# Loads of shrinking size through one ring, in a row-maximum kernel

## The chip, the core and the metric

The kernel runs on one core of one Trainium2 chip. The metric is the device time of one execution in microseconds (us). Several executions are made of each kernel, and kernels that are compared run in turns on the same chip. The profile of an execution gives its *span*, from the first to the last instruction of the program; in the runs below the time is 1.7 to 2.0 us longer than the span of the same execution. Where the text says faster or slower, it means that the 95% interval leaves out 1, or it compares medians and says so.

## The reference

```python
def setup_inputs():
    batch, seq, dim = 32, 512, 1024
    return {"x": np.random.randn(batch, seq, dim).astype(np.float32)}

def reference(x):
    return np.max(x, axis=-1).astype(np.float32)
```

The input is 67 MB, the output 64 KB: 16,384 rows of 1024 floats, each reduced to its maximum. A kernel lays 128 rows in a line on each of the 128 partitions, so "one row" below means one row on every partition, 128 x 4 KB = 0.52 MB, and the whole work is 128 such rows.

## The kernel before

```python
    GB = 4
    GT = 2
    TAIL_ROWS = 16
    ...
    bulk = ctx.enter_context(tc.tile_pool(name="bulk", bufs=10))
    tailp = ctx.enter_context(tc.tile_pool(name="tailp", bufs=5))
    ...
    for c in range(NB):                      # 28 loads of four rows
        b = c * GB
        xc = bulk.tile([P, GB, D], mybir.dt.float32)
        nc.sync.dma_start(out=xc, in_=xr[:, b:b + GB, :])
        nc.vector.reduce_max(out=res[:, b:b + GB], in_=xc, axis=mybir.AxisListType.X)

    nc.scalar.dma_start(out=out_r[:, :SPLIT], in_=res[:, :SPLIT])

    for t in range(NT):                      # 8 loads of two rows
        b = SPLIT + t * GT
        xt = tailp.tile([P, GT, D], mybir.dt.float32)
        nc.sync.dma_start(out=xt, in_=xr[:, b:b + GT, :])
        nc.vector.reduce_max(out=res[:, b:b + GT], in_=xt, axis=mybir.AxisListType.X)

    nc.scalar.dma_start(out=out_r[:, SPLIT:], in_=res[:, SPLIT:])
```

The sync engine (SP) issues the loads, the vector engine (DVE) takes the maxima, the scalar engine (ACT) issues two stores. The framework adds the semaphore waits.

## Time and profile before

| | before |
|---|---|
| time, median of runs | 166.98 us (166.93 to 167.51) |
| span of the profiled execution | 166.5 us |
| DVE busy | 141.4 us, 85% |
| load queue busy | 95.7% of sixteen DMA engines |
| loads | 36: 28 of four rows, 8 of two |

The page and the views that matter are shown in the prediction. One more pair of lines is needed for what follows. It is from the timeline of the vector engine in the kernel before (start in us, duration, engine and line, operation, and in brackets how long the engine had stood idle and what it waited for):

```profile
22.90 4.42 DVE L47 TENSOR_REDUCE res<-xc 128x4 f32<-128x4096 f32 x1 [0.47 <-DMA xc<-in_x_dram]
...
28.43 4.42 DVE L47 TENSOR_REDUCE res<-xc 128x4 f32<-128x4096 f32 x1 [1.11 <-DMA xc<-in_x_dram]
```

The usual wait for a four-row load is 0.47 us. The load that is taken up at 28.43 came 0.64 us late: a stall of the load stream. There is a second one of 0.86 us at 58.61. The packet records of the trace show what a stall is (below, a packet counts as stalled that takes 0.25 us longer than the usual one of its size): at 23.1 to 23.7 us, eight of the sixteen DMA engines each need 0.6 to 0.8 us longer than usual for one packet, and at 51.1 to 51.6 us eight need up to 1.8 us longer (the records kept here do not number the engines; eight late packets at once are read as eight engines). The other eight have no late packet. At the first stall the first engine to land stays on time (27.12 us, one usual load of 4.90 us after the 22.22 of the load before); at the second, when the sixteen stood 1.25 us apart, it comes 0.35 us late (56.85, where 51.60 and 4.90 give 56.50), and which engines were struck the records do not say. The load was taken up only when its slowest engine had landed: at 28.43, with the last landing at 28.40, and at 58.61, with the last at 58.59.

### The profile page before, as it was taken

What the parts mean: (1) busy time and instruction counts of PE and PEld (TensorE: products, weight loads), DVE (VectorE), ACT (ScalarE), POOL (GpSimd) and SP (SyncE); (2) the same over time, 40 slices, a digit from 0 to 9 for tenths busy, and PEclk for the clock granted to TensorE, in tenths of its full rate; (3) what the DMA queues carried; (4) which work ended last, traced back from release to release, by engine and by line L of the source; (5) the groups of instructions that cost most, each with busy time, mean ns of one, the idle gap of its engine ahead of it and who ended that gap; (6) DMA issues with size and microseconds to landing.
All of it is one profiled execution on the core that took longest, in us unless ns stands there. A gap on an engine that the chain in (4) does not pass through costs nothing.

```text
span 166.5 us, 142 instructions
## 1 busy us (share of the span) xinstructions
DVE 141.4 (85%) x36; POOL 0.2 (0%) x4
## 2 busy tenths in 40 slices
DVE  0098887898888798888898888899888889999994
POOL 0000000000000000000000000000000000000000
DMA  5999999999999999999999999999999999999950
GB/s 189 429 441 429 429 394 425 433 437 429 433 421 354 425 433 429 429 429 429 433 421 429 429 429 437 417 429 433 429 433 421 425 433 411 425 417 423 421 222 2
DMA packets 5472, 67.18 MB, mean 404 GB/s; under 512 B 864, under 2 KB 864, under 8 KB 864
## 3 DMA queue, kind: packets, MB, share of 16 engines
q1 hardware_dynamic: 5184, 67.11, 95.7%
q10 hardware_dynamic: 288, 0.07, 0.2%
HBM read 67.11 MB, written 0.07 MB: 403 GB/s over the span
## 4 chain that ended last, share of the span: by engine, by line
DMA 89%; DVE 8%; SPq 1%; issue 0%
DMA xc<-in_x_dram 84%; DMA xt<-in_x_dram 5%; DVE res L59 5%; DVE res L47 3%; SPq L46 1%
## 5 line engine op out<-in xcount | busy, mean ns | idle before, releaser
L47 DVE TENSOR_REDUCE res<-xc 128x4 f32<-128x4096 f32 x28 | 123.8, 4420 | 22.5 <-DMA xc<-in_x_dram 22.5
L59 DVE TENSOR_REDUCE res<-xt 128x2 f32<-128x2048 f32 x8 | 17.8, 2280 | 0.2 <-DMA xt<-in_x_dram 0.2
L80 POOL MEMSET const-bfloat16-1.0<- 128x1 bf16 x1 | 0.1, 103 | 0.0
L80 POOL MEMSET const-uint8-127<- 128x1 uint8 x1 | 0.1, 103 | 0.0
L80 POOL MEMSET const-float32-1.0<- 128x1 f32 x1 | 0.1, 100 | 0.0
L80 POOL MEMSET const-float32-0.0<- 128x1 f32 x1 | 0.1, 99 | 0.2 <-issue 0.2
## 6 DMA issues: line engine op xcount, KB each, us to landing
xc<-in_x_dram SPq DMA_DIRECT2D x28, 2048.0 KB, 39.1
xt<-in_x_dram SPq DMA_DIRECT2D x8, 1024.0 KB, 23.5
out_dram<-res ACTq DMA_DIRECT2D x1, 56.0 KB, 6.8
out_dram<-res ACTq DMA_DIRECT2D x1, 8.0 KB, 1.4
```

Source lines behind the costliest of these rows:

```text
L46: nc.sync.dma_start(out=xc, in_=xr[:, b:b + GB, :])
L47: nc.vector.reduce_max(out=res[:, b:b + GB], in_=xc, axis=mybir.AxisListType.X,)
L59: nc.vector.reduce_max(out=res[:, b:b + GT], in_=xt, axis=mybir.AxisListType.X,)
L80: nc = _bacc.Bacc("TRN2", target_bir_lowering=False, num_devices=1)
```

## The change

The intent is to issue fewer and larger loads while there is much to do, and ever smaller ones towards the end, so that little is left to reduce when the last bytes arrive. All loads go through one tile of 46 rows used as a ring.

```diff
+ROWS = [10, 13, 12, 10, 9, 8, 7, 7, 6, 5, 5, 4, 4, 3, 3, 3, 3, 2, 2, 2, 2, 2, 1, 1, 1, 1, 1]
+RING = 46
...
-    bulk = ctx.enter_context(tc.tile_pool(name="bulk", bufs=10))
-    tailp = ctx.enter_context(tc.tile_pool(name="tailp", bufs=5))
+    ring = once.tile([P, RING, D], F32)
+    res = once.tile([P, I], F32)
+    part = once.tile([P, 2], F32)
...
+    for g in ROWS:
+        if at + g > RING:
+            at = 0
+        xc = ring[:, at:at + g, :]
+        nc.sync.dma_start(out=xc, in_=xr[:, b:b + g, :])
+        nc.vector.reduce_max(out=res[:, b:b + g], in_=xc, axis=X)
+        at += g
+        b += g
+        if not stored and b >= I - 16:
+            stored = b
+            nc.scalar.dma_start(out=out_r[:, :b], in_=res[:, :b])
...
+    for h in range(2):
+        xh = ring[:, at, h * H:(h + 1) * H]
+        nc.sync.dma_start(out=xh, in_=xr[:, b, h * H:(h + 1) * H])
+        nc.vector.reduce_max(out=part[:, h:h + 1], in_=xh, axis=X)
+    nc.vector.tensor_tensor(
+        out=res[:, b:b + 1], in0=part[:, 0:1], in1=part[:, 1:2],
+        op=mybir.AluOpType.max,
+    )
+    nc.scalar.dma_start(out=out_r[:, stored:], in_=res[:, stored:])
```

(The two old loops are cut from the diff; they stand above.)

More of the change, by code (lines that the diff above doesn't have):

```diff
@@ L7 @@
 from concourse._compat import with_exitstack
+F32 = mybir.dt.float32
+ROWS = [10, 13, 12, 10, 9, 8, 7, 7, 6, 5, 5, 4, 4, 3, 3, 3, 3, 2, 2, 2, 2, 2, 1, 1, 1, 1, 1]
+RING = 46
 @with_exitstack
@@ L18 @@
     P = 128
+    X = mybir.AxisListType.X
     xf = x.flatten_outer_dims()
     N, D = xf.shape
-    assert N % P == 0
+    H = D // 2
     I = N // P
@@ L28 @@
     out_r = bass.AP(tensor=of.tensor, offset=of.offset, ap=[[I, P], [1, I]])
-    GB = 4
-    GT = 2
-    TAIL_ROWS = 16
-    NB = (I - TAIL_ROWS) // GB
-    NT = TAIL_ROWS // GT
-    SPLIT = I - TAIL_ROWS
-    bulk = ctx.enter_context(tc.tile_pool(name="bulk", bufs=10))
-    tailp = ctx.enter_context(tc.tile_pool(name="tailp", bufs=5))
-    respool = ctx.enter_context(tc.tile_pool(name="res", bufs=1))
-    res = respool.tile([P, I], mybir.dt.float32)
-    for c in range(NB):
-        b = c * GB
-        xc = bulk.tile([P, GB, D], mybir.dt.float32)
-        nc.sync.dma_start(out=xc, in_=xr[:, b:b + GB, :])
-        nc.vector.reduce_max(
-            out=res[:, b:b + GB],
-            in_=xc,
-            axis=mybir.AxisListType.X,
-        )
-    nc.scalar.dma_start(out=out_r[:, :SPLIT], in_=res[:, :SPLIT])
-    for t in range(NT):
-        b = SPLIT + t * GT
-        xt = tailp.tile([P, GT, D], mybir.dt.float32)
-        nc.sync.dma_start(out=xt, in_=xr[:, b:b + GT, :])
-        nc.vector.reduce_max(
-            out=res[:, b:b + GT],
-            in_=xt,
-            axis=mybir.AxisListType.X,
-        )
-    nc.scalar.dma_start(out=out_r[:, SPLIT:], in_=res[:, SPLIT:])
+    once = ctx.enter_context(tc.tile_pool(name="once", bufs=1))
+    ring = once.tile([P, RING, D], F32)
+    res = once.tile([P, I], F32)
+    part = once.tile([P, 2], F32)
+    b = at = 0
+    stored = 0
+    for g in ROWS:
[9 more added lines that the diff above has]
+            nc.scalar.dma_start(out=out_r[:, :b], in_=res[:, :b])
+    assert b == I - 1 and at + 1 <= RING
+    for h in range(2):
[7 more added lines that the diff above has]
+    nc.scalar.dma_start(out=out_r[:, stored:], in_=res[:, stored:])
 _INS = ['x']
```

## The prediction

> **What bounds the kernel now.** I read the page first, then the timeline of the vector engine (DVE), then the chain of waits and the groups. Of the page, the share of each engine, the strip of slices and the queue:
>
> ```profile
> DVE 141.4 (85%) x36; POOL 0.2 (0%) x4
> ...
> DMA  5999999999999999999999999999999999999950
> GB/s 189 429 441 429 429 394 425 433 437 429 433 421 354 425 433 429 429 429 429 433 421 429 429 429 437 417 429 433 429 433 421 425 433 411 425 417 423 421 222 2
> ...
> q1 hardware_dynamic: 5184, 67.11, 95.7%
> ```
>
> The load queue is full from the second slice to two before the last, at about 429 GB/s, so the load stream sets the time; the DVE has only some 25 us to spare over the whole. Two slices (394 and 354 GB/s) show short stalls. The groups give the price of a reduce:
>
> ```profile
> L47 DVE TENSOR_REDUCE res<-xc 128x4 f32<-128x4096 f32 x28 | 123.8, 4420 | 22.5 <-DMA xc<-in_x_dram 22.5
> L59 DVE TENSOR_REDUCE res<-xt 128x2 f32<-128x2048 f32 x8 | 17.8, 2280 | 0.2 <-DMA xt<-in_x_dram 0.2
> ```
>
> Two rows more cost 4420 - 2280 = 2140 ns, so a row is 1.07 us and an instruction has a fixed 0.14 us (4.42 - 4 x 1.07). The timeline gives the rhythm (start, duration, then in brackets the idle time before):
>
> ```profile
> 132.03 4.42 DVE L47 TENSOR_REDUCE res<-xc 128x4 f32<-128x4096 f32 x1 [0.47 <-DMA xc<-in_x_dram]
> 136.92 4.42 DVE L47 TENSOR_REDUCE res<-xc 128x4 f32<-128x4096 f32 x1 [0.47 <-DMA xc<-in_x_dram]
> 141.82 4.42 DVE L47 TENSOR_REDUCE res<-xc 128x4 f32<-128x4096 f32 x1 [0.48 <-DMA xc<-in_x_dram]
> 146.16 15.47 DVE L59 TENSOR_REDUCE res<-xt 128x2 f32<-128x2048 f32 x7
> ...
> 161.80 2.29 DVE L59 TENSOR_REDUCE res<-xt 128x2 f32<-128x2048 f32 x1 [0.17 <-DMA xt<-in_x_dram]
> 164.12 0.34 ACTq L65 DMA_DIRECT2D out_dram<-res  x1
> ```
>
> In the bulk the DVE waits 0.47 us for each load, so a four-row load takes 4.895 us. In the tail it runs seven two-row reduces without a gap: a backlog, because a four-row reduce holds it 4.42 us while a two-row load lands in about 2.5 us. It has just worked that off when the last load lands at 161.78. Then follow 2.29 us of reduce and 2.4 us of store and ending (164.09 to 166.5). The chain says the same, and what paces the issue of loads:
>
> ```profile
> 102.70 39.10 DMA xc<-in_x_dram
> 141.80 0.02 issue
> 141.82 4.42 DVE res L47
> 146.24 6.59 DVE res L59 x3
> 152.84 0.02 issue
> 152.85 8.93 DMA xt<-in_x_dram
> 161.78 0.02 issue
> 161.80 2.29 DVE res L59
> ```
>
> A load issued at 102.70 lands 39.10 us later, which is 8 x 4.89: eight loads are in flight, and a new one is issued when the load eight before it lands. The end is thus last landing (161.8), plus whatever the DVE has left then (2.29), plus 2.4.
>
> [...]
>
> **The price of a load.** The last four-row load lands at 141.80 and eight two-row loads later it is 161.78: 19.98 / 8 = 2.4975 us each (1.049 MB in that time is 420 GB/s). From 4r + f = 4.895 and 2r + f = 2.4975 follows r = 1.199 us a row and f = 0.10 us a load. All 36 loads are 128 x 1.19875 + 36 x 0.10 = 157.04 us; the last one is taken up at 161.80, so start, latency and the two stalls are 4.76 us. The stalls show as DVE waits of 1.11 us before 28.43 and 1.33 before 58.61, against 0.47: 0.64 + 0.86 = 1.5 us of the 4.76. I keep them.
>
> **The change, part by part.**
> 1. Loads: 27 + 2 = 29 in place of 36. The bytes stay, so 7 x 0.10 = 0.7 us goes, and the last landing is taken up at 161.80 - 0.70 = 161.10. I chose to let f hold for 52 KB and 2 KB pieces per partition, outside the two sizes measured.
> 2. Start of the DVE: the first reduce waits for ten rows, six more than now, so it starts near 8.24 + 6 x 1.2 = 15.4 in place of 8.24. From there 29 reduces back to back are 128 x 1.07 + 29 x 0.05 = 138.4 us (0.05 because a back-to-back one starts before the end of the one before: 2.28 us long, but one each 2.19). That could end at 153.8, so the late start costs nothing; it must only not leave a backlog.
> 3. Backlog: the DVE keeps up from group k to k+1 where 1.07 g(k) + 0.14 stays below 1.199 g(k+1) + 0.10, that is where a size is at least about 0.9 of the one before. The list does that or repeats a size until the backlog is gone. Reckoned through the list, the waits for the DVE stay under 0.8 us; the five two-row loads take up 0.3 us each (2.4975 against 2.19) and clear the backlog of the 3-to-2 step. So the last two-row reduce starts at landing: 161.10 - 5 x 1.299 - 2 x 0.699 = 153.21, and ends at 155.49.
> 4. Tail: one-row loads come each 1.299 us, one-row reduces take 1.07 + 0.14 = 1.21 and 1.12 back to back. Five of them start at 155.40, 156.52, 157.64, 158.76 and 159.88, each behind its landing. The half rows: reduce 0.535 + 0.14 = 0.675, 0.585 back to back. They start at 161.00 and 161.59, the second 0.49 after its data, and end at 162.26. The maximum of the two parts follows: [...] 162.45. So 1.35 us follow the last landing in place of 2.29: of the ideal gain of a half-row end [...] one third is lost to backlog.
> 5. Stores: the first still covers 112 rows, the last 16. The 2.4 us stay.
> 6. Ring: 46 rows in place of 50. For each load I compared the reckoned moment its rows are read out, and that of the landing eight before it, with the moment when the stream would reach it: the smallest spare time is 9.7 us, for the last half row (released by the landing of the twenty-first load, near 150.8, wanted near 160.4). No load should come late.
>
> Sum: DVE end 164.09 to 162.45, 1.64 us less; 166.98 - 1.64 = 165.3 us, about 1.0% faster.
>
> **Rivals.**
> A. The price per load does not fall with their number (larger pieces gain nothing, or pieces of 4 and 2 KB cost more than 0.10 extra). Then the last landing stays at 161.8 and only about 0.9 us of tail is won: 166.0. For it: f comes from two sizes only. Against: in the trace nothing; it is a line through two points that I lengthen.
> B. The DVE becomes the bound at the end: the taper is tuned tight, and if a short reduce had 0.25 us fixed in place of 0.14, seven short ones add 0.11 each, 0.8 us: 166.1. Against: [...] the fixed part that is left over from two sizes should hold for a third.
> C. The stalls shrink, move or fall together. They cost 1.5 us; without them 163.8. For it: the stream's order changes wholly. Against: nothing in the profile ties them to a load or an instruction, and three runs agree within 0.6 us.
> D. The ring is one tile: if overlaps of its parts were tracked as a whole, every load would wait for the reduce before it, loads and reduces would alternate, and the time would be near 157 + 139 = 296. For it: one allocation. Against: the kernel before already writes one result tile in parts and stores a part of it at 146.27 while reduces of later rows are still to come.
>
> **Range and chances.** A and B together would give 166.9, one alone about 166.0; C alone 163.8; a start with larger first pieces may win or lose some tenths. I take 164.2 to 166.4. Faster by over 2% needs 163.6, which takes C and more: 0.06. Slower takes D or an unseen wait: 0.03. Within 2%: 0.91.
>
> **What would show it.** 29 loads and load share near 95%; first reduce near 15.4; four-row and larger groups at 1.07 us a row; the last landing near 161.1; one-row reduces without gaps in the last 7 us, and 1.3 to 1.4 us from last landing to the end of the maximum; last store issued near 162.5. I am wrong if the last landing is not earlier by 0.5 to 0.9 us, if a load waits for the ring so that the strip of slices has a hole, if the stalls are gone, or if the DVE still has a row or more left at the last landing.

162.26 us for the end of the second half row and 0.19 for the maximum with its waiting gave the 162.45, and so the 1.35 us after the last landing, the 1.64 us of gain and the 165.3 us. (In the trace of the change it is 0.20 us from the end of the second half row to the end of the maximum, 162.21 to 162.41.)

## The result, and the profile after

| | before | after |
|---|---|---|
| time, median | 166.98 us (166.93 to 167.51) | 166.44 us (165.94 to 166.67) |
| span of the profiled execution | 166.5 us | 164.7 us |
| DVE busy | 141.4 us | 139.5 us |
| loads | 36 | 29 |

The ratio after to before is 0.9954 (95% interval 0.9934 to 0.9975). Such a ratio is the mean time of one kernel's runs over that of the other's of the same rounds, so it is not quite the ratio of the medians. The change is faster by half a per cent where one per cent was predicted, and 166.44 lies just above the range of 164.2 to 166.4.

The spans tell another story than the times: 1.8 us between the two profiles, 0.5 us between the medians. The four executions of the changed kernel have spans of 164.7, 164.6, 164.2 and 164.9 us, each 1.7 to 1.8 us below its time. By that distance the profiled execution of the kernel before, with its span of 166.5, would have a time near 168.2 us, more than the slowest of its listed times. The profile that I predicted from was thus of an unusually slow execution (an inference from the distance), and the span of a median one would be near 165.2 us.

These lines are from the page of the changed kernel (busy time by engine; the 40 slices; the queue of the loads):

```profile
DVE 139.5 (85%) x30; POOL 0.2 (0%) x4
...
DMA  6998999999989999999999999999999999999960
GB/s 199 438 467 376 453 465 453 436 406 394 469 388 467 444 430 430 408 438 425 439 432 425 426 431 419 428 438 409 438 430 421 427 421 421 420 418 421 408 260 2
...
q1 hardware_dynamic: 4176, 67.11, 95.8%
```

No slice has a hole, so the ring never made a load late. The early slices swing because few packets of 40 and 52 KB fall into a slice of 4.1 us (their medians in this trace are 1.51 and 1.97 us, so two or three an engine); the row of busy shares above them stays at 8 and 9 tenths. Next the timeline of the vector engine, its start and its end:

```profile
15.82 10.82 DVE L48 TENSOR_REDUCE res<-ring 128x10 f32<-128x10240 f32 x1 [15.82 <-DMA ring<-in_x_dram]
31.56 14.02 DVE L48 TENSOR_REDUCE res<-ring 128x13 f32<-128x13312 f32 x1 [4.91 <-DMA ring<-in_x_dram]
...
160.94 1.27 DVE L59 TENSOR_REDUCE part<-ring 128x1 f32<-128x512 f32 x2
162.25 0.16 DVE L60 TENSOR_TENSOR res<-part 128x1 f32<-128x1 f32 x1
162.44 0.34 ACTq L64 DMA_DIRECT2D out_dram<-res  x1
```

The first reduce starts at 15.82, 0.4 us later than predicted; the vector work ends at 162.41, where 162.45 was predicted. And the last part of the chain that ended last (start, length, what):

```profile
133.17 19.92 DMA ring<-in_x_dram
153.08 0.02 issue
153.11 7.92 DVE res L48 x6
161.02 1.20 DVE part L59 x2
162.22 0.02 issue
162.25 0.16 DVE res L60
```

From the landing of the last two-row load at 153.08 to the end, the chain is vector work alone: six reduces, two halves, one maximum, without a gap. The last half row is complete at 160.74, 1.67 us before the vector work ends.

So the profile agrees with the prediction to 0.04 us at the end of the vector work, and yet the gain is half of what was predicted. That is possible because two errors cancel in this one trace. It has only 0.66 us of stall (two packets of the nine-row load are late, and its slowest landing with them), where the prediction carried 1.5 us of stalls over. Something else must have cost what the missing stalls saved.

### The profile page after: what moved, and what is told of

It reads as the page before. It is cut to its first block, busy times and chain, and to the rows that moved or that the text cites. A ratio compares the mean times of both kernels' runs of the same rounds, so it can differ in the third digit from the quotient of the medians.

```text
span 164.7 us, 118 instructions
## 1 busy us (share of the span) xinstructions
DVE 139.5 (85%) x30; POOL 0.2 (0%) x4
## 3 DMA queue, kind: packets, MB, share of 16 engines
q1 hardware_dynamic: 4176, 67.11, 95.8%
## 4 chain that ended last, share of the span: by engine, by line
DMA 70%; DVE 28%; issue 0%
DMA ring<-in_x_dram 70%; DVE res L48 27%; DVE part L59 1%; DVE res L60 0%
## 5 line engine op out<-in xcount | busy, mean ns | idle before, releaser
L48 DVE TENSOR_REDUCE res<-ring 128x2 f32<-128x2048 f32 (+11 forms) x27 | 138.1, 5165 | 22.9 <-DMA ring<-in_x_dram 22.7
L59 DVE TENSOR_REDUCE part<-ring 128x1 f32<-128x512 f32 x2 | 1.3, 676 | 0.0
```

Source lines behind the costliest of these rows:

```text
L48: nc.vector.reduce_max(out=res[:, b:b + g], in_=xc, axis=X)
L59: nc.vector.reduce_max(out=part[:, h:h + 1], in_=xh, axis=X)
```

## The experiments

Theory: without stalls the change gains some 0.9 us and not 1.6, because the start of the stream and the large loads cost more than my line said; the stalls come on top and blur it. Rival: the gain is as predicted, but large loads draw stalls of their own that take it back. Each kernel below, but for the repetitions of the two kernels themselves, is the changed kernel with another list of sizes; those whose list ends with a whole row also lack the two half rows and the maximum of them. Landing times of the single DMA engines are from the semaphore updates in the trace.

### Both kernels again, and each half of the change alone (one chip)

`e1_before` is the kernel before, unchanged.

> The kernel before once more, as the control, to see what its usual execution looks like. The profile that I predicted from had a span of 166.5 us with two stalls (0.64 + 0.86 us) of half of the DMA engines. Theory S (the stalls of that profile are not usual): the time is again 167.0 us, the span about 165.2 (1.75 us less than the time, as in all runs of the changed kernel), a trace has at most about 0.3 us of late landings, the last load lands near 160.4. Rival M (the stalls are usual and the distance of time and span is another for this kernel): span 166.4 to 166.5, the stalls at the same places, last landing 161.8.

Measured: ratio 1.0003, spans 165.5 to 166.4; the trace (166.0) has again two stalls of eight engines each, at 22.9 and at 62.2 us. The first makes later loads land almost 1.0 us late. The second strikes while the engines stand 1.45 us apart, and then they are only 0.84 apart: it hits the engines that were ahead and costs the end nothing. The last load lands at 161.25. The thirteenth load lands at 67.82, where 8.12 of the first and 12 x 4.895 give 66.86, so 0.96 us is what the stalls cost. Taking it off gives 160.29; the first profile gives 161.78 - 1.50 = 160.28. The two agree, so the kernel before **without stalls** has its last landing at 160.28 and a span of 160.28 + 2.29 + 2.40 = 164.97 us. Both theories were half right: stalls are usual, at 23 us even at the same place, but less costly than in the first profile (median span 165.8, so about 0.8 over 164.97).

`e1_after` is the changed kernel again.

> The changed kernel once more. Theory S: its trace held one engine that fell behind by 0.66 us at 65 to 68 us (the load of nine rows: spread of the sixteen engines' landings from 0.89 to 1.56 us) and an early spread of 0.93 against 0.67 us; if that is usual for it, spans are 164.2 to 164.9 again and the last load lands near 160.7 to 160.8, and the true gain is 0.5 to 0.8 us. Rival: that stall was chance; then this trace has none, a span near 164.0, and the list of spans scatters over 0.7 us or more.

Measured: ratio 0.9948 (0.9918 to 0.9979); spans 164.3 to 166.0. The rival expected such scatter, but also a trace without a stall, and this execution (166.0) has one at 62.9 us (five engines, again in the nine-row load) and one at 75.1 us (eight engines, 1.5 to 1.9 us each, in the eight-row load), and its engines end 2.4 us apart. The early spread is there again, 0.90 us.

`e1_tail` keeps four-row loads to row 112 and takes the new tail alone.

```diff
-ROWS = [10, 13, 12, 10, 9, 8, 7, 7, 6, 5, 5, 4, 4, 3, 3, 3, 3, 2, 2, 2, 2, 2, 1, 1, 1, 1, 1]
+ROWS = [4] * 28 + [2, 2, 2, 2, 2, 1, 1, 1, 1, 1]
```

> The new tail alone: loads of four rows to row 112, then 2,2,2,2,2,1,1,1,1,1 and two halves, in the ring of 46. If the backlog reckoning holds, the backlog of the four-row loads is not worked off in so short a tail, the DVE ends as late as before: the same time as before, within 0.3 us (the last landing is 0.3 us later for the five loads more, and the end of the vector work 0.1 us later). If the tail is what gains, 1.0 to 1.4 us less than before.

Measured: ratio 1.0033 (1.0005 to 1.0062), slower by 0.5 us between the means and 0.3 between the medians; the trace has two stalls. Its timeline shows why the fine tail gains nothing:

```profile
142.44 21.02 DVE L48 TENSOR_REDUCE res<-ring 128x4 f32<-128x4096 f32 x11 [0.50 <-DMA ring<-in_x_dram]
...
163.37 1.27 DVE L59 TENSOR_REDUCE part<-ring 128x1 f32<-128x512 f32 x2
```

From the landing of the last four-row load the vector engine runs eleven reduces and then the halves without a gap. 22.4 us after that landing it is done (142.44 to 164.84). In the kernel before it was 22.3 us (141.82 to 164.09). With that backlog before them, the smaller loads did not end sooner.

`e1_bulk` has the large loads alone, with the old tail and no half rows.

```diff
-... 3, 3, 3, 3, 2, 2, 2, 2, 2, 1, 1, 1, 1, 1]      (and the two half rows)
+... 3, 3, 3, 3, 2, 2, 2, 2, 2, 2, 2, 2]
```

> The large loads alone: the first 17 loads of the change (10,13,...,3,3,3,3), then eight loads of two rows as before, in the ring of 46. By the price of a load: 11 loads fewer than before, 0.9 to 1.1 us less stream, and the end follows it by 0.9 to 1.1 us. If large loads bring their own delay (engines that start or fall behind unevenly), the gain is under 0.3 us and the spread of the landings is above 1.2 us.

Measured: ratio 0.9959 (0.9934 to 0.9984), 0.7 us less between the means. The trace has no stall at all, and its chain ends

```profile
160.04 0.02 issue
160.07 2.29 DVE res L48
```

so the last landing is 160.04, only 0.24 us before the 160.28 of the kernel before without stalls. By the prediction's line, eleven loads fewer should have given 1.1 us. Two things took the rest. The stream starts late: the first ten rows land at 15.99, where the landing of the first four rows at 8.22 plus six rows at 1.2 us give some 15.4. And the line itself is off. The two-row loads of this trace are taken up 2.48 us apart (each was waited for, as the brackets say):

```profile
152.64 2.29 DVE L48 TENSOR_REDUCE res<-ring 128x2 f32<-128x2048 f32 x1 [0.17 <-DMA ring<-in_x_dram]
155.12 2.29 DVE L48 TENSOR_REDUCE res<-ring 128x2 f32<-128x2048 f32 x1 [0.20 <-DMA ring<-in_x_dram]
157.60 2.29 DVE L48 TENSOR_REDUCE res<-ring 128x2 f32<-128x2048 f32 x1 [0.19 <-DMA ring<-in_x_dram]
160.07 2.29 DVE L48 TENSOR_REDUCE res<-ring 128x2 f32<-128x2048 f32 x1 [0.18 <-DMA ring<-in_x_dram]
```

The prediction had 2.4975, a mean over eight loads of the kernel before. One of the eight took 2.62 us (it lands at 151.87), the others 2.46 to 2.50. Each of the twenty traces has such a late two-row load, or two that are a little late, while the 144 packets of the first store pass or just after (in the changed kernel the packets start from 147.5 to 150.4 us, and the late load lands at 150.75). In the eight-row kernel below, whose first store is the latest of all, the late load is the latest too (154.71). That the store delays it is read from this coincidence; no run leaves the store out.

With 2.485 us for a two-row load, 4r + f = 4.895 and 2r + f = 2.485 give r = 1.205 us a row and f = 0.075 us a load. That fits loads of all whole rows. Between successive landings in the changed kernel (in brackets the line of 1.205 and 0.075, then the prediction's): 15.73 us for thirteen rows (15.74, 15.68), 14.53 for twelve (14.54, 14.49), 12.12 for ten (12.13, 12.09), 8.51 for seven (8.51, 8.49), 1.28 for one (1.28, 1.30). So in these landings the large loads cost the stream nothing of their own, but for the first one. In this kernel eleven loads fewer are worth 0.83 us, and the late start takes 0.54 of it (15.99 against 8.22 + 6 x 1.205 = 15.45). The 0.29 us that remain are close to the 0.24 measured.

### The start, the end, and both together (another chip)

`e2_start46` cuts the first load in two.

```diff
-ROWS = [10, 13, 12, ...
+ROWS = [4, 6, 13, 12, ...
```

> The first load of ten rows cut into four and six; all else as the change. In the three traces with a ten-row first load it lands at 15.74 to 15.99 us, where my line put 15.35, and the sixteen engines' landings of it are 0.90 to 1.13 us apart against 0.61 to 0.67 for a four-row first load. Theory H (a large first piece costs the start about 0.4 us, for good, since each engine keeps its lag): ten rows are there at 15.4 to 15.5, spread about 0.65, and all later landings 0.3 us earlier than in the change where no stall is; end 0.3 us earlier. Rival (the start is the same for any size, large pieces are slow throughout): ten rows at 15.8 plus 0.1 for the load more, end 0.1 us later.

Measured: ratio 0.9885 (0.9857 to 0.9913). Its timeline:

```profile
8.10 4.42 DVE L48 TENSOR_REDUCE res<-ring 128x4 f32<-128x4096 f32 x1 [8.10 <-DMA ring<-in_x_dram]
15.38 6.55 DVE L48 TENSOR_REDUCE res<-ring 128x6 f32<-128x6144 f32 x1 [2.86 <-DMA ring<-in_x_dram]
...
31.12 14.02 DVE L48 TENSOR_REDUCE res<-ring 128x13 f32<-128x13312 f32 x1 [9.19 <-DMA ring<-in_x_dram]
45.81 12.95 DVE L48 TENSOR_REDUCE res<-ring 128x12 f32<-128x12288 f32 x1 [0.67 <-DMA ring<-in_x_dram]
```

Ten rows are there at 15.36 instead of 15.8, although there is one load more, and thirteen rows later it is 31.09 instead of 31.53. The engines' own landings of the first ten rows:

```
first load            ten rows landed (last engine)      engines apart
ten rows  (6 traces)  15.74 15.78 15.80 15.81 15.97 15.99   0.87 to 1.13
4 + 6     (5 traces)  15.34 15.36 15.36 15.51 15.53         0.45 to 0.74
```

Theory H, that ten rows as one load come about 0.4 us later than as two, agrees with all eleven traces (with the repetitions below). Why is not shown. The sixteen engines begin about 1 us apart, and their first packets take longer than later ones: in the first two profiles on average 0.65 us longer with the 40 KB packets of the change and 0.47 with the 16 KB of the kernel before, which is less than half of the 0.4 us. Nor does all of the gain last. In this trace it was lost again in the loads of twelve and ten rows: row 45 is there at 58.16 us, in the changed kernel at 58.18. So the low ratio of this run is not shown to come from the start. Over the five traces with a split first load, row 45 lands at 57.74 to 58.17, in the six others at 58.13 to 58.40: of 0.43 us on average, 0.27 are left.

`e2_nohalf` keeps the last row whole.

```diff
-    for h in range(2):  ...  nc.vector.tensor_tensor(...)
+ROWS = [..., 1, 1, 1, 1, 1, 1]
```

> The last row as one load and one reduce, in place of two halves and a maximum; all else as the change. Theory B (in the last 7.7 us the vector engine is the bound: six one-row reduces run without a gap from the landing of the last two-row load): from that landing to the end of the vector work 9.30 us in the change becomes 2.29 + 6 x 1.126 + small = 9.05, so 0.25 us less, although the last reduce is twice as long. Rival (the end follows the last landing): the work after the last landing grows from 1.35 to 1.3 or more and the last load lands the same, so no gain or 0.2 us later.

Measured: ratio 0.9894 (0.9871 to 0.9917). The last two-row load lands at 152.42, then

```profile
152.44 9.05 DVE L48 TENSOR_REDUCE res<-ring 128x2 f32<-128x2048 f32 x7 [0.17 <-DMA ring<-in_x_dram]
161.52 0.34 ACTq L56 DMA_DIRECT2D out_dram<-res  x1
```

9.05 us to the end of the vector work, against 9.30 in the change (153.11 to 162.41), as theory B said to the hundredth. (The time fell by more: 166.10 us, against 166.92 for the change in later rounds on the same chip. What is over 0.25 us of that is not explained; the executions of the change scatter by 1.2 us there.) A half row *lengthens* the end by 0.25 us, because the vector engine is the bound there: two short reduces and a maximum take 1.39 us in the change (161.02 to 162.41), and the one whole reduce in their place takes 1.13 here (the last piece of this run's chain). This trace has no stall, and so gives the change without stalls: the same to 152.42, then 0.02 + 9.30 + 2.32 (the end of its own trace, 162.41 to 164.73), a span of 164.06 us.

`e2_best` does both and refines the taper: 4,6,13,12,10,9,8,7,7,6,5,5,4,4,4,3,3,3,2,2,2,2 and seven of one.

> Both, and a finer taper: 4,6,13,12,10,9,8,7,7,6,5,5,4,4,4,3,3,3,2,2,2,2 and seven of one. By the reckoning with the measured prices and no stall: end 0.7 us before the change and 1.6 us before the kernel before, so a ratio to before near 0.990 to 0.991 (the change 0.995). If start and half rows don't matter, 0.995 as the change.

Measured: ratio 0.9842 (0.9822 to 0.9863), median 165.29 us against 167.94, better than expected; spans 163.4 to 163.7. Its end:

```profile
151.21 10.17 DVE L48 TENSOR_REDUCE res<-ring 128x2 f32<-128x2048 f32 x8 [0.20 <-DMA ring<-in_x_dram]
161.41 0.34 ACTq L56 DMA_DIRECT2D out_dram<-res  x1
```

`e2_ring` has the old sizes in the new ring.

```diff
+ROWS = [4] * 28 + [2] * 8
```

> The old sizes (28 loads of four, 8 of two) in the new ring of 46 rows: the form alone. Loads are paced by the landing eight before, so the same time as before, within 0.3 us. On stalls: the three traces with four-row loads had half of the engines late at 23 us (0.5 to 0.9 us), the three with large loads not there. If it belongs to four-row loads, it is here too, at 23.0 to 23.7 us; if it was chance, it is elsewhere or gone.

Measured: ratio 1.0003 (0.9983 to 1.0023). The ring itself does nothing. The trace has two stalls of eight engines again, but the first at 13.4 us and not at 23.

### The change beside its variants, and three-row loads (the same chip again)

Of the thirteen executions of the kernel before in this group, eleven are those of the group above.

> The changed kernel, now in the same rounds as its variants. Without stalls its span is reckoned at 164.0 to 164.1 (first landing 15.8, last two-row landing 152.4, 9.30 us of vector work, 2.35 to the end), against 164.95 for the kernel before: a gain of 0.9 us that stalls blur. Expected ratio 0.993 to 0.996. If its 0.995 of two chips was bad luck with stalls, it comes out at 0.989 like the two half variants.

Measured: ratio 0.9937 (0.9915 to 0.996), as expected; so the 0.995 of the two chips before was not bad luck.

> The split first load once more, beside the change. First look: ten rows at 15.36 as theory H said, but 0.3 us of it lost again in the loads of twelve and ten rows. If H holds: first ten rows at 15.3 to 15.5 again, spread under 0.75, and a time 0.2 to 0.5 us under the change of the same rounds. If the loss in the loads after it belongs to the split: that loss is here again and the time is within 0.2 us of the change.

Measured: ratio 0.989 (0.9864 to 0.9916), median 166.07 against 166.92 for the change: 0.85 us less, more than the start can explain. Ten rows at 15.51 and no loss in the loads of twelve and ten rows this time; but fifteen late packets in the nine-row load at 60 us. The direction is as theory H has it; the size of the gain is not settled by it.

> The best version once more, on another chip and beside the change: ratio to before 0.983 to 0.988, and 0.6 to 1.3 us under the change of the same rounds; list of spans narrower than that of before.

Measured: ratio 0.9872 (0.9848 to 0.9895), 1.3 us under the change (the chip was the same as in the last rounds, not another).

`e3_three`, sizes `[3] * 37 + [2] * 8 + [1]`:

> Loads of three rows (37), then eight of two and one of one, in the ring, for the stalls: all four traces with loads of four rows hold two stalls of eight engines each (mean loss 0.7 to 1.2 us an engine), all between 13 and 63 us; of six traces with large loads one holds two, one a stall of two engines, four none over 0.5 us. Without stalls I reckon 1.0 us more stream than before (ten loads more) and a span of 165.2 to 165.8. If small loads draw stalls, the trace holds two or more and the median span is 0.7 or more above that; if the stalls are chance, none to two at other places, and the time 0.3 us over before.

Measured: ratio 0.9962 (0.9944 to 0.998), median 167.33 against 168.01, and spans within 165.4 to 165.7. The trace has no stall. Its slices:

```profile
DMA  5999999999999999999999999999999999999960
GB/s 181 428 428 425 430 430 428 428 428 425 428 428 428 428 425 428 428 425 428 428 425 428 428 428 425 428 428 428 425 428 425 428 428 415 418 422 423 426 281 4
```

Beside the strip of the kernel before, with its 394 and 354, nothing dips. Ten loads *more* than before, and yet 0.7 us faster. The last load lands at 161.07, 0.79 us after the 160.28 of the kernel before without stalls, and ten loads at 0.075 us are 0.75. So the price per load is there, but the kernel before pays more for stalls, which this trace does not have.

### What draws the stalls (a third chip)

> One row first, then 27 loads of four, one of three, eight of two: four-row loads whose pieces no longer begin at multiples of four rows. Theory P (place: the stalls need pieces of 16 KB that begin at multiples of 16 KB): no stall of eight engines in the trace, spans 165.0 to 165.4, narrow. Theory Z (the size and rhythm of a four-row load): two stalls again between 13 and 63 us, median span 165.7 to 166.2. Theory F (chance): anything between, other places.

Sizes `[1] + [4] * 27 + [3] + [2] * 8`. Measured: ratio 0.9978 (0.9945 to 1.0011), spans scattered from 164.7 to 166.7; one stall of eight engines at 14.4 to 14.8 us, and a single late packet at 16.8. Theory P falls here: moved by one row, four-row loads still stall. Theory Z, which asked for two stalls, is not confirmed either.

> 22 loads of five rows and nine of two. Three-row loads gave no stall and spans within 0.3 us. Theory P: pieces of 20 KB mostly begin off the multiples: at most small stalls, spans 165.1 to 165.5 (reckoned 165.2 without stalls). Theory that longer pieces draw stalls: two, median span 166 or more.

Sizes `[5] * 22 + [2] * 9`. Measured: ratio 0.9949 (0.9928 to 0.997), spans 165.1 to 165.3, no stall; the 165.2 reckoned.

> 14 loads of eight rows, then eight of two. Two questions. Backlog: an eight-row reduce takes 8.7 us and a two-row load lands in 2.49, so the vector engine ends 22 reduces without a gap from the landing of the 14th load: span 168.1 to 168.6 although the last load lands near 159.4 without stalls, 0.9 earlier than before; if the end followed the stream, the span would be near 164.1. Stalls: P expects them here (multiples of 32 KB), F none in particular.

Sizes `[8] * 14 + [2] * 8`. Measured: ratio 1.0134 (1.0112 to 1.0157), slower, spans 168.1 to 168.6 as reckoned; the last load lands at 159.63 (159.4 expected). There is no stall at all, which is again against P. The backlog is plain to see:

```profile
129.94 8.69 DVE L48 TENSOR_REDUCE res<-ring 128x8 f32<-128x8192 f32 x1 [1.03 <-DMA ring<-in_x_dram]
139.66 26.23 DVE L48 TENSOR_REDUCE res<-ring 128x8 f32<-128x8192 f32 x9 [1.03 <-DMA ring<-in_x_dram]
165.92 0.34 ACTq L56 DMA_DIRECT2D out_dram<-res  x1
```

In the bulk the vector engine waits 1.03 us for each load, so it is not busy. After the last eight-row load it runs nine reduces in one piece, and ends at 165.89. The fewest loads of all kernels make the slowest one, because nothing is left of the 1.03 us when sizes fall from eight to two.

The last three ran in the same rounds, on yet another chip.

> 5, seven of 8, 7,6,6,6,5,5,4,4,3,3,3,2,2,2,2 and seven of 1, whole rows: the best version without pieces over eight rows. Reckoned without stalls 0.1 us behind the best version (span 163.4 against 163.3). If stalls go with the size of the pieces (fours in the bulk, nines and twelves in the large loads; none with threes, fives and eights): no stall in the trace, spans within 0.4 us at 163.3 to 163.7, and a median at or under the best version's. If stalls are chance for all but fours: as scattered as the best version, median 0.1 above it.

Sizes `[5, 8, 8, 8, 8, 8, 8, 8, 7, 6, 6, 6, 5, 5, 4, 4, 3, 3, 3, 2, 2, 2, 2] + [1] * 7`. Measured: ratio 0.9888 (0.9861 to 0.9915); spans 163.5 to 164.7, so wider than expected, and two late packets in an eight-row load at 28 us. That stalls go with the size of the pieces is thus not confirmed.

> The best version again, for the same rounds: spans 163.3 to 164.6 scattered by stalls in the nine- or twelve-row load, ratio to before 0.984 to 0.988.

Measured: ratio 0.9891 (0.9855 to 0.9927), outside what I expected by a little; spans 163.4 to 165.1, eight engines stalled at 60 us in the nine-row load.

> The change in the same rounds as both: ratio to before 0.993 to 0.996, and 1.0 to 1.3 us over the best version.

Measured: ratio 0.993 (0.9906 to 0.9955), median 166.5 against 165.98 for the best version: 0.5 us, not 1.0 to 1.3. The trace has the same stall of eight engines in the nine-row load at 60 us.

What the stalls are is **not settled**. Found: all four traces of uniform four-row loads hold two stalls of eight engines, the shifted one a single one. The traces of uniform loads of three, five and eight rows (one each) hold none, and their runs lie within 0.5 us. Kernels with the falling sizes hold anything from none to two. All begin before 77 us. Chance alone does not look likely either: in seven of the eleven traces with a nine-row load, that load has late packets (1 to 15), all between 59.5 and 66 us, and two of the four uniform four-row traces stall at 62 us. Stalls that depended on time alone would strike three- and five-row loads as well, of which there is one trace each; place in memory alone is ruled out by the shifted and the eight-row kernels. What makes eight engines wait together, no run shows.

## Why the prediction was right or wrong

**What bounds the kernel.** Right. The stream fills the queue (95.7% and 95.8% of sixteen engines before and after), and the end is the last landing plus what the DVE has left. The bulk kernel, without a stall, follows its stream (160.07 + 2.29), and the eight-row kernel shows the other end of it.

**Loads and start: the step that failed.** "So start, latency and the two stalls are 4.76 us", "I keep them", and the last landing "at 161.80 - 0.70 = 161.10" with f held "for 52 KB and 2 KB pieces". Without the 1.5 us of stalls that is a last landing of 159.60 and, with the predicted tail, an end of the vector work at 160.95. Measured without stalls: 152.44 + 9.30 = 161.74. The 0.8 us between are three terms:

```
                                            predicted   measured   difference
ten rows landed                             15.41       15.85      +0.44   (mean of the six traces above)
from there to row 122 (no stall)            136.36      136.61     +0.25   (112 x 1.19875 + 21 x 0.10; 15.81 to 152.42)
from row 122 to the end of the DVE          9.24        9.32       +0.08   (153.21 to 162.45; 0.02 + 9.30)
```

The first term is the start: ten rows as the first load land 0.4 us later than the line has them. The second is f, the price of a load. The prediction's line went through a mean of 2.4975 us for a two-row load, in which one was late. The line through 2.485 gives 136.54 us for these 112 rows in 21 loads, and the one late load adds 0.12 (2.63 + 2.46 against 2 x 2.485): 136.66, beside 136.61 measured. So the mechanism, fewer loads and thus less stream, was right, and its sizes were off: seven loads fewer are worth 7 x 0.075 = 0.53 us and not 0.70, and the large first load takes 0.4 of that back. Without its stall of 0.66 us the last load of the change lands at 160.08, only 0.20 us before the 160.28 of the kernel before. Of the 1.64 us, 0.9 us remain: 164.97 to 164.06 without stalls. The four comparisons of the change gave 0.9954, 0.9948, 0.9937 and 0.993, which of 167 to 168 us is 0.8 to 1.2 us.

**The stalls.** "I keep them" was also wrong as a rule, though it cancels in a difference if both kernels stall alike. On the chips of the experiments the kernel before has median spans of 165.8 to 166.2, some 0.8 to 1.2 us over its span without stalls, and the changed kernel of 164.8 to 165.2, some 0.7 to 1.1 over its own. (That all of this is stalls is taken over from the profiled executions; the others left no trace.) In the rounds of the record the kernel before stood only about 0.3 us above it (an estimate: its median time less 1.75 us) and the change 0.6 (164.65). By this estimate that is how a gain of 0.9 became 0.54 between the medians, and it took the time out of the range by 0.04 us, so a little luck would have hidden the error. The range was too narrow for a term of 1.5 us whose scatter I had seen only once.

**Start of the DVE, backlog, tail.** Right. The late start (15.82 us in place of 8.24) costs nothing. The backlog rule held in the change (the last two-row reduce starts 0.03 us after its landing), and where it was broken on purpose. One-row reduces took 1.21 us and came each 1.126 back to back (1.21 and 1.12 predicted), which is 0.14 and 0.06 us over the 1.07 of a row; half rows took 0.676 (0.675), the maximum 0.159 us. Small loads landed faster than reckoned, 1.28 us for one row and 0.63 for half a row (1.299 and 0.699 predicted), 410 and 416 GB/s beside 422 for a two-row load of 2.485 us. It gained nothing: 1.67 us of work follow the last landing in place of 1.35, since the DVE is the bound from row 122 on. I had written that a third of the gain of a half row is lost to backlog; in truth half rows lose 0.25 us against a whole one, a comparison that I did not make. Of the four signs of being wrong that the prediction named, three came: the last landing was 1.04 us earlier (161.78 to 160.74; more than 0.9, since less was stalled), more than half of the 1.5 us of stalls was gone, and more than a row of work (1.67 us) was left at the last landing.

**Stores and ring.** Right: 2.32 us after the vector work (2.4), no hole in the strip, and the ring alone gives 1.0003.

**Rivals.** A held in part: the price per load does fall with their number, but it is 0.075 us and not 0.10, and a large first load takes most of the gain back. B did not happen: the fixed part of a one-row reduce is 0.14 us (1.208 less the 1.07 of a row). C held in part: stalls do differ with the sizes, which I had argued against because nothing in one profile tied them to a load. D is ruled out by the ring kernel.

## What to carry to other kernels

When loads shrink towards the end, compare each reduce with the load *after* it: here a row took 1.07 us to reduce and 1.205 to load, so the vector engine keeps up only while a size is about nine tenths of the one before or more (an estimate from these two figures; where sizes fell from eight to two it ended 6.26 us after the last landing, 159.63 to 165.89). Stop shrinking the last pieces where two short instructions take longer than one whole one: here two half rows and their maximum ended 9.30 us after the last two-row landing, a whole row 9.05. Begin with a small load: here the first ten rows came 0.43 us sooner as four and six, of which 0.27 were left at row 45. Those first loads, a whole last row and a finer taper together gave ratios of 0.984 to 0.989 where the change as made gave 0.993 to 0.995. Draw a line of costs through loads that nothing else disturbs: one late load among eight raised the price of a load from 0.075 to 0.10 us. Before building on a term in one profile, such as a stall, see several executions: half of a predicted gain of 1% was within what a stall does.
